# A two-layer hybrid backbone on one core: the mixed features are loaded into the slots of the split weights instead of the slots of the raw weights

## The chip, the core and the metric

The kernel runs on one core of one Trainium2 chip, as one program. The metric is the device time of one execution in microseconds (us), and the time of a kernel is the median over several executions. The engines of the core are called PE (matrix multiplication, with PEld for its weight loads), DVE (vector), ACT (scalar), POOL and SP. Each works through its own instructions strictly in the order in which the program holds them, and each instruction waits at the head of its engine for the semaphores that it needs. DMA transfers are issued by SP and ACT from that same order, so a transfer that has to wait holds up whatever stands behind it on that engine.

## The reference: what is computed

512 latent tokens and 256 context tokens of width 1024 go through two layers. Cut to what matters here:

```
for layer in range(DEPTH):                      # DEPTH = 2
    a   = modulate(rms_norm(h, norm1_g[layer]), shift1, scale1)
    p   = a @ w_in[layer]                       # one projection, columns shared out to three groups
    d   = diff_mixer(p ...)                     # differential attention, 256 columns
    q   = gqa_mixer(p ...)                      # grouped-query attention, 384 columns
    n   = gdn_mixer(p ...)                      # gated DeltaNet in both directions, 384 columns
    h   = h + gate1 * (concatenate([d, q, n]) @ w_out[layer])
    h   = h + gate2 * swiglu(modulate(rms_norm(h, norm2_g[layer]), shift2, scale2),
                             ffn_w_gu[layer], ffn_w_down[layer])
return rms_norm(h, final_norm_g)
```

In layer 0 the context tokens go through the same steps with their own modulation; in layer 1 they only serve as keys and values, so only the 512 latent tokens are mixed, projected and passed on. The change touches the step between the three mixers and `@ w_out`.

## The kernel before, in words

Activations lie transposed, as eight blocks of 128 features by tokens, numbered k = 0 to 7: k 0 and 1 come from the differential attention, k 2 to 4 from the grouped-query attention, k 5 to 7 from DeltaNet. Every large product is made in three passes over pairs of fp32r parts: a value is split into a high part (a copy, on ACT, L185) and a low part (value minus high part, on DVE, L161), and `mm3` (L194 on) multiplies hi by hi and hi by lo for every k and then lo by hi for every k (matmuls on L188; transposes are on L191).

**The mixers.** `mixers` runs a list of items in a fixed order for each layer, PLAN (L38): attention steps (`a`), DeltaNet inversions, scan steps and outputs (`p`, `s`, `o`), and near the end `x0`, which calls `mixed`. The order of the five attention pairs is HORD = (2, 0, 3, 1, 4), so k = 4 is finished last. `attn_post` (L1235) sends each finished pair to a DRAM buffer `mixd` (tile `OT`, issued by SP); `gdn_out` (L927) sends k 5 to 7 there (tile `z2`). The last pair, k 4, does not go through DRAM: it is transposed by PE into `otr` and split from there.

**The reload.** `mixed` (L958 to L970) loads the seven other blocks (`early_k`: k 0, 1, 2, 3, 5, 6, 7) from `mixd` into tiles `mx`, by SP (L152), and splits each into `mhi` and `mlo`. The split is made for each part of the tokens: in layer 0 the parts are 512 and 256 tokens, in layer 1 they are two of 256, so each `mx` has two copies on ACT and two subtractions on DVE.

**The region of the weights.** `mixed` also opens (L961, `open_a`, L1422) the region from which the out-projection takes its weights: slots of 128 by 1024 floats, 3 with the tag `raw`, 4 with `hi`, 4 with `lo`. A slot that is asked for again waits for the last reader of its old content. `wunit` (L212) takes one slot of each tag, loads 512 KB of weights into `raw` (by ACT's queue, L156), copies it to `whi` (ACT, L185) and subtracts to `wlo` (DVE, L161). In the kernel before, the seven `mx` tiles go round the three `raw` slots, so that the fourth `mx` waits for the first to be split, and the first weights `w_o` come after them in the same slots.

**The out-projection.** `outproj` makes eight column tiles `ops` for each part, each of 24 products (seven blocks of `mx` with three products each, then three for k 4), and adds each to the residual stream `h`, which has been in DRAM meanwhile and is loaded back by SP behind the `mx` loads. Two PSUM banks take turns, so a third tile waits until the first has been added to `h` on DVE. The norm, the gate and up products (`guc`, `gu`) and the down products (`dps`) follow.

The order on each engine is not that of the Python text: a scheduler goes over the whole program with its own estimates of time, and puts each engine's instructions in the order in which it finds them ready, with priorities for weights and for the mixers.

Of the kernel before, what the change touches and what calls it, by code (L numbers as in the profile page):

```python
# [10 lines left out]
F32 = mybir.dt.float32  # L11
# [83 lines left out]
class Net:  # L95
# [862 lines left out]
    def mixed(self, l, side, parts):  # L958

        self.G2.close()  # L960
        self.G.close()  # L961
        self.open_a(l + 1, side)
        tags = "ce" if l == DEPTH - 1 else "ac"
        self.mhi, self.mlo = ([self.ablock(n, *p[:2], t) for p, t in zip(parts, tags)] for n in ("mhi", "mlo"))
        t0 = min(p[0] for p in parts)
        for kt in self.early_k(l):
            x = self.W.slot("mx", F32, "raw")
            self.dma(x[:, t0:TOK], self.mixd[kt][:, t0:TOK])
            for a, n, _ in parts:
                self.split(self.at(self.mhi, kt, a, n), self.at(self.mlo, kt, a, n), x[:, a:a + n])  # L970
# [695 lines left out]
```

## Time and profile before

| | kernel before |
|---|---|
| time, median of 3 runs | 2184.11 us (2183.25 to 2184.77) |
| the profiled execution: its time | 2187.43 us |
| its span in the trace | 2185.6 us |
| busy: PE, PEld | 92%, 77% of the span |
| busy: DVE, ACT, POOL | 61%, 38%, 24% |
| mean granted clock of PE | 0.943 |

A page of the profile shows one execution. Times are in us from the start of the span; "x7" after an instruction means that seven like it stand in one row. In a list in order of time, the square brackets hold how long the engine stood idle before the row, and what released it; a duration is from start to end, and matmuls overlap, so a steady rate is read from the distance of the starts. The granted clock is given as a share of full speed: 1.00 is 2.4 GHz, 0.50 is 1.2 GHz, and a value between is a stretch with some of each.

### The profile page before, as it was taken

How to read it: one execution, taken by the hardware profiler on the slowest of the kernel's cores; microseconds unless marked ns; L12 is line 12 of the kernel's file. 1: busy time of each engine (PE TensorE's matmuls, PEld its weight loads, DVE VectorE, ACT ScalarE, POOL GpSimd, SP SyncE). 2: the span in 40 equal slices, each digit the busy share in tenths (PEclk: the TensorE clock that was granted, in tenths of full speed). 3: DMA queues.
4: the chain of work that ended last, by engine and by line, in shares of the span. 5: the costliest groups of instructions: out<-in, count | busy, mean ns of one | idle time of the engine just before them, and what ended most of it. 6: DMA issues, size and time to landing. Idle time of an engine off the chain costs nothing. (4 is left out here: it accounts for less than half of the span.)

```text
span 2185.6 us, 36979 instructions
## 1 busy us (share of the span) xinstructions
PE 2020.9 (92%) x14786; PEld 1672.6 (77%) x14786; DVE 1325.2 (61%) x2223; ACT 823.8 (38%) x1609; POOL 525.0 (24%) x768
## 2 busy tenths in 40 slices
PE   7999877998889999999999989977899799999998
PEld 3788766776668888888888888865676598888887
DVE  6755774575845747565757457687767664443444
ACT  5433315464744321212122344423475653222223
POOL 2403579331014100000000350367323030000002
PEclk9999987698999999999999989987798999999999
DMA  8354434221062324343424411444212242222321
GB/s 296 121 176 132 156 109 113 47 73 35 26 227 78 116 87 154 110 131 102 155 91 140 134 56 48 133 127 125 51 47 60 86 165 77 100 85 92 106 98 61
DMA packets 167596, 236.46 MB, mean 108 GB/s; under 512 B 75328, under 2 KB 109248, under 8 KB 167424
## 3 DMA queue, kind: packets, MB, share of 16 engines
q10 hardware_dynamic: 46160, 144.92, 20.2%
q1 hardware_dynamic: 121264, 89.18, 13.4%
q8 instruction: 116, 1.90, 0.3%
q14 instruction: 56, 0.46, 0.1%
HBM read 198.00 MB, written 36.04 MB: 107 GB/s over the span
## 5 line engine op out<-in xcount | busy, mean ns | idle before, releaser
L185 ACT ACTIVATE whi<-raw 128x1024 fp32r<-128x1024 f32 (+4 forms) x246 | 220.7, 912 | 499.6 <-PE dps L188 207.3
L161 DVE TENSOR_TENSOR wlo<-raw,whi 128x1024 fp32r<-128x1024 f32 (+4 forms) x236 | 250.1, 1074 | 222.1 <-ACT whi L185 221.3
L188 PE MATMUL gu<-ahi,wlo 128*128 128x512 f32 x672 | 264.0, 393 | 1.1 <-DVE wlo L161 1.1
L188 PE MATMUL gu<-ahi,whi 128*128 128x512 f32 x672 | 263.6, 392 | 0.0
L188 PE MATMUL dps<-acth,whi 128*128 128x512 f32 (+1 forms) x560 | 186.6, 348 | 0.4 <-DVE h L179 0.2
L188 PE MATMUL dps<-acth,wlo 128*128 128x512 f32 (+1 forms) x560 | 185.7, 346 | 0.0
L188 PE MATMUL gu<-alo,whi 128*128 128x512 f32 x672 | 168.9, 392 | 0.0
L179 DVE SCALAR_TENSOR_TENSOR junk<-adaw,cb 128x1024 bf16<-128x1024 f32 x112 | 136.8, 1222 | 37.6 <-DMA adaw<-ada_t 36.6
L188 PEld LDWEIGHTS gu<-ahi,wlo 128*128 128x128 f32 x672 | 126.5, 188 | 28.3 <-DVE wlo L161 1.5
L188 PE MATMUL tps<-whi,ahi 128*128 128x512 f32 (+4 forms) x368 | 137.9, 379 | 11.1 <-ACT dq L185 7.2
L188 PEld LDWEIGHTS gu<-alo,whi 128*128 128x128 f32 x672 | 126.3, 188 | 27.6
L179 DVE SCALAR_TENSOR_TENSOR h<-dps,md,h 128x512 f32<-128x512 f32 (+1 forms) x128 | 80.6, 633 | 109.6 <-PE dps L188 109.3
L188 PEld LDWEIGHTS gu<-ahi,whi 128*128 128x128 f32 x672 | 126.5, 188 | 26.7
L188 PE MATMUL tps<-wlo,ahi 128*128 128x512 f32 (+4 forms) x368 | 138.3, 376 | 2.6 <-DVE wlo L161 2.4
L161 POOL TENSOR_TENSOR md<-md,adab 128x2 f32<-128x2 f32 x56 | 32.0, 572 | 439.5 <-DVE junk L179 439.5
L188 PE MATMUL tps<-whi,alo 128*128 128x512 f32 (+4 forms) x368 | 137.3, 373 | 0.0
L1161 DVE TENSOR_REDUCE nm<-S 128x1 f32<-128x768 f32 (+1 forms) x140 | 117.0, 844 | 32.6 <-PE S L188 31.4
L182 ACT ACTIVATE P<-S,nm 128x768 f32<-128x768 f32 (+1 forms) x140 | 114.0, 815 | 51.7 <-DVE nm L1161 46.1
L161 POOL TENSOR_TENSOR sqc<-sqc 128x256 f32<-128x256 f32 x35 | 35.4, 1012 | 397.8 <-ACT sqc L182 397.4
L188 PE MATMUL dps<-actl,whi 128*128 128x512 f32 (+1 forms) x560 | 124.3, 346 | 0.0
L188 PEld LDWEIGHTS dps<-acth,whi 128*128 128x128 f32 x560 | 105.4, 188 | 15.6 <-DVE h L179 0.4
L188 PEld LDWEIGHTS dps<-acth,wlo 128*128 128x128 f32 x560 | 105.7, 189 | 14.3
(295 smaller groups left out, 4629.0 us busy)
## 6 DMA issues: line engine op xcount, KB each, us to landing
raw<-w_u ACTq DMA_DIRECT2D x88, 512.0 KB
adaw<-ada_t ACTq DMA_DIRECT2D x56, 512.0 KB
adaw<-ada_p ACTq DMA_DIRECT2D x24, 512.0 KB
raw<-w_o ACTq DMA_DIRECT2D x24, 512.0 KB
raw<-w_d ACTq DMA_DIRECT2D x44, 256.0 KB
raw<-w_d ACTq DMA_DIRECT2D x32, 320.0 KB
adaq<-ada_q SPq DMA_DIRECT2D x16, 512.0 KB
raw<-w_t ACTq DMA_DIRECT2D x16, 512.0 KB
```

The source lines that it names most:

```text
L161: (eng or self.v).tensor_tensor(out=out, in0=a, in1=b, op=op)
L179: self.v.scalar_tensor_tensor(out=out, in0=a, scalar=sc, in1=b, op0=op0, op1=op1, **k)
L182: self.s.activation(out=out, in_=in_, func=func, **k)
L185: self.s.activation(out=out, in_=in_, func=AF.Copy, **k)
L188: self.t.matmul(out, lhsT, rhs, start=start, stop=stop)
L1161: self.v.tensor_reduce(out=nm, in_=pin, axis=AX.XY if nk == 768 else AX.X, op=ALU.max, negate=True)
```

## The change

`mixed` asks for its seven slots by another tag: in turn `hi` and `lo`, where it asked for `raw`. So k 0, 2, 5 and 7 fill the four `hi` slots and k 1, 3 and 6 fill three of the four `lo` slots, and no `mx` waits for another. The three `raw` slots are empty, and the first three weight loads of the out-projection find them so. In exchange the first `whi` and `wlo` tiles come behind `mx` tiles: the second `whi` follows k 2 and the second `wlo` k 1, the third `whi` k 5, the third `wlo` k 3. The number of instructions is the same on every engine.

```
     def mixed(self, l, side, parts):
...
-        for kt in self.early_k(l):
-            x = self.W.slot("mx", F32, "raw")
+        for i, kt in enumerate(self.early_k(l)):
+            x = self.W.slot("mx", F32, ("hi", "lo")[i % 2])
             self.dma(x[:, t0:TOK], self.mixd[kt][:, t0:TOK])
             for a, n, _ in parts:
                 self.split(self.at(self.mhi, kt, a, n), self.at(self.mlo, kt, a, n), x[:, a:a + n])
```

Other slots move the scheduler's estimates, and with them the order on all engines: besides the places below, some 600 rows on PE and some 300 each on DVE and ACT stand elsewhere than before in layer 1, most of them in the DeltaNet and attention work between about 1490 and 1740 us of the trace; POOL's order is the same.

First the loads of layer 1 on SP, at the end of the mixers; rows with - stood there before, rows with + stand there now. In the names, `mx_17566` is k 0, `mx_17572` k 1, `mx_17578` k 2, `mx_17584` k 3, `mx_17590` k 5, `mx_17596` k 6, `mx_17602` k 7, and each `OT` is a finished attention pair on its way to DRAM (`mixd1`).

```order
 L152 DMA mx_17566<-mixd1_14856 128x512
+L152 DMA mx_17578<-mixd1_14856 128x512
+L152 DMA mx_17590<-mixd1_14856 128x512
+L152 DMA mx_17602<-mixd1_14856 128x512
 L152 DMA mixd1_14856<-OT_17052 128x512
 L152 DMA mixd1_14856<-OT_17518 128x512
 L152 DMA mx_17572<-mixd1_14856 128x512
-L152 DMA mx_17578<-mixd1_14856 128x512
 L152 DMA mx_17584<-mixd1_14856 128x512
-L152 DMA mx_17590<-mixd1_14856 128x512
 L152 DMA mx_17596<-mixd1_14856 128x512
-L152 DMA mx_17602<-mixd1_14856 128x512
```

The four blocks that go to the `hi` slots moved ahead of the two waits for attention pairs; k 1, 3 and 6 stay behind the second pair, which is k 1 itself.

The same moment of layer 1 on ACT, whose queue issues the weights. Before, the first weight load stood some sixty rows later; in the changed order it reads:

```order
L185 ACTIVATE PT_16863<-pt_16869 128x384
L156 DMA raw_17779<-w_o 128x1024
L156 DMA raw_17813<-w_o 128x1024
L156 DMA raw_17848<-w_o 128x1024
L185 ACTIVATE OTs_16889<-pv_16876 128x128
L185 ACTIVATE PT_16913<-pt_16914 128x384
L182 ACTIVATE P_16978,Z_16974<-S_16975,nm_16979 128x768
L182 ACTIVATE P_16985,Z_16974<-S_16982,nm_16986 128x768
L185 ACTIVATE mhi_17534<-mx_17566 128x256
```

And the end of the mixers on ACT, where the out-projection starts. Before:

```order
L185 ACTIVATE OTs_17724<-pv_17711 128x128
L185 ACTIVATE mhi_17540<-mx_17596 128x256
L185 ACTIVATE mhi_17548<-mx_17596 128x256
L156 DMA raw_17779<-w_o 128x1024
L185 ACTIVATE mhi_17541<-mx_17602 128x256
L185 ACTIVATE mhi_17549<-mx_17602 128x256
L185 ACTIVATE mhi_17538<-otr_17728 128x256
L156 DMA raw_17813<-w_o 128x1024
L156 DMA raw_17848<-w_o 128x1024
L185 ACTIVATE whi_17780<-raw_17779 128x1024
```

and in the changed kernel:

```order
L185 ACTIVATE PT_17698<-pt_17704 128x384
L185 ACTIVATE whi_17814<-raw_17813 128x1024
L185 ACTIVATE mhi_17547<-mx_17590 128x256
L185 ACTIVATE mhi_17540<-mx_17596 128x256
L185 ACTIVATE OTs_17724<-pv_17711 128x128
L185 ACTIVATE mhi_17548<-mx_17596 128x256
L185 ACTIVATE mhi_17541<-mx_17602 128x256
L185 ACTIVATE mhi_17549<-mx_17602 128x256
L156 DMA raw_17918<-w_o 128x1024
L185 ACTIVATE whi_17849<-raw_17848 128x1024
L185 ACTIVATE whi_17884<-raw_17883 128x1024
```

The first three weight loads are gone from here, the first `whi` was made in the middle of the attention, and the second `whi` stands among the last `mx` copies; the loads that stand here now are those of later tiles.

On PE in layer 0, at the same junction, `ops` is a column tile of the out-projection, `otr` the transposes of the last attention pair (k 4), `pv` the end of its attention. Before:

```order
L191 MATMUL otr_6845<-ident_92,O_6429 128x128 x4
L188 MATMUL pv_6836<-PT_6817,gV_3481 64x128
L191 MATMUL otr_6852<-ident_92,O_6429 128x128
L188 MATMUL pv_6836<-PT_6829,gV_3481 64x128
L188 MATMUL pv_6836<-PT_6817,gV_3481 64x128
L188 MATMUL pv_6836<-PT_6829,gV_3481 64x128
L188 MATMUL ops_6920<-mhi_6639,whi_6915 128x512
L191 MATMUL pv_6836<-ident_92,OTs_6841 128x128
L188 MATMUL ops_6920<-mhi_6639,wlo_6916 128x512
```

and in the changed kernel, at the end of the tile's 14 products with `mhi`:

```order
L188 MATMUL ops_6920<-mhi_6646,whi_6915 128x512
L188 MATMUL ops_6920<-mhi_6646,wlo_6916 128x512
L191 MATMUL otr_6845<-ident_92,O_6429 128x128 x4
L191 MATMUL otr_6852<-ident_92,O_6429 128x128
L191 MATMUL pv_6836<-ident_92,OTs_6841 128x128
L188 MATMUL ops_6920<-mlo_6655,whi_6915 128x512
```

In layer 0 the fourteen products moved ahead of the last pair's transposes; before, five of the six `otr` transposes came ahead of the tile and the last one behind its fifth `mlo` product. In layer 1 PE now runs two column tiles without k 4 and makes the k 4 products of both behind them, where each tile had its own at its end.

## Rows read from the trace of the kernel before

**Rows 1.** Chain that ended last, layer 1: start, us, what.

```profile
1730.81 2.00 DMA mixd<-OT
1732.82 2.61 DMA mx<-mixd
...
1740.80 6.90 DMA raw<-w_o
...
1748.81 1.24 DVE wlo L161
...
1750.09 29.73 PE ops L188 x228
...
1825.85 44.62 PE gu L188 x192
```

**Rows 2.** PE in order of time, start of the out-projection of layer 1.

```profile
1740.86 0.33 PE L191 MATMUL otr<-ident,O 128*128 128x128 f32 x1 [0.38 <-DVE O L161]
1748.83 0.58 PE L188 MATMUL ops<-mhi,whi 128*128 128x256 f32 x1 [7.65 <-ACT whi L185]
1750.09 0.58 PE L188 MATMUL ops<-mhi,wlo 128*128 128x256 f32 x1 [0.68 <-DVE wlo L161]
...
1755.06 0.28 PE L188 MATMUL ops<-mhi,whi 128*128 128x256 f32 x1
...
1757.94 0.28 PE L188 MATMUL ops<-mhi,whi 128*128 128x256 f32 x1
```

**Rows 3.** ACT in order of time, same place (ACTq: DMA issues of its queue).

```profile
1735.46 0.72 ACT L185 ACTIVATE mhi<-mx 128x256 fp32r<-128x256 f32 x2 [3.25 <-DMA mx<-mixd]
...
1736.61 1.33 ACT L185 ACTIVATE mhi<-mx 128x256 fp32r<-128x256 f32 x4
1738.00 0.49 ACT L185 ACTIVATE PT<-pt 128x384 f32<-128x384 f32 x1
...
1739.83 0.26 ACT L185 ACTIVATE OTs<-pv 128x128 f32<-128x128 f32 x1
...
1742.00 1.02 ACTq L156 DMA_DIRECT2D raw<-w_o  x2
1747.72 1.06 ACT L185 ACTIVATE whi<-raw 128x1024 fp32r<-128x1024 f32 x1 [5.38 <-DMA raw<-w_o]
```

**Rows 4.** Stretches: length, busy by engine, granted PE clock, DMA share, GB/s.

```profile
1490.00:1540.00 50.00, 34.47 (x532) 26.93 (x533) 35.99 (x74) 22.84 (x53) 30.39 (x48) 0.76 0.53 137
1540.00:1600.00 60.00, 51.81 (x816) 38.12 (x816) 40.87 (x82) 28.96 (x68) 20.79 (x25) 0.77 0.19 39
...
1688.00:1700.00 12.00, 9.90 (x72) 6.54 (x72) 10.42 (x19) 9.23 (x22) 0.00 (x0) 1.00 0.08 23
...
1736.00:1741.00 5.00, 3.03 (x25) 1.87 (x21) 3.44 (x10) 3.60 (x12) 0.00 (x0) 1.00 0.59 190
1741.00:1749.00 8.00, 0.35 (x2) 0.17 (x1) 1.96 (x6) 2.62 (x7) 0.00 (x0) 0.52 0.93 338
1749.00:1755.00 6.00, 5.32 (x24) 5.03 (x25) 3.73 (x4) 2.06 (x3) 0.00 (x0) 0.51 0.88 290
```

**Rows 5.** ACT in order of time, the same junction of layer 0.

```profile
611.32 0.94 ACT L185 ACTIVATE mhi<-mx 128x512 fp32r<-128x512 f32 x2 [2.25 <-DMA mx<-mixd]
...
627.75 0.38 ACT L185 ACTIVATE mhi<-otr 128x256 fp32r<-128x256 f32 x1 [1.85 <-PE otr L191]
```

**Rows 6.** PE in order of time, the out-projection of layer 0.

```profile
621.95 0.50 PE L188 MATMUL ops<-mhi,whi 128*128 128x512 f32 x1 [0.69 <-ACT whi L185]
...
623.21 0.50 PE L188 MATMUL ops<-mhi,wlo 128*128 128x512 f32 x1 [0.65 <-DVE wlo L161]
...
627.44 0.27 PE L191 MATMUL otr<-ident,O 128*128 128x128 f32 x1
...
635.66 0.47 PE L188 MATMUL ops<-mhi,whi 128*128 128x512 f32 x1 [1.28 <-DVE h L179]
```

**Rows 7.** DVE in order of time, layer 0: the residual sums.

```profile
634.76 1.41 DVE L179 SCALAR_TENSOR_TENSOR h<-ops,md,h 128x512 f32<-128x512 f32 x2 [3.53 <-DMA h<-h]
```

**Rows 8.** SP's DMA issues in order of time, layer 0.

```profile
627.74 4.95 SPq L152 DMA_DIRECT2D h<-h  x8
```

More of the change, by code (lines that the diff above doesn't have):

```diff
@@ L965, in mixed @@
         t0 = min(p[0] for p in parts)
-        for kt in self.early_k(l):
-            x = self.W.slot("mx", F32, "raw")
+        for i, kt in enumerate(self.early_k(l)):
+            x = self.W.slot("mx", F32, ("hi", "lo")[i % 2])
             self.dma(x[:, t0:TOK], self.mixd[kt][:, t0:TOK])
```

## The prediction

> **What bounds the kernel now.** I read the chain of waits first, for the work that sets the end. In layer 1 it leaves the engines at the end of the mixers: from the write of the last attention pair through DRAM, over the `mx` loads, to the load of the first out-projection weights, which takes 6.90 us, then the low part of those weights, and only then PE [rows 1]. From there PE carries the chain on, and at 1825.85 it is still PE, in the gate and up products [rows 1]. So what is saved ahead of 1750.09 should reach the end. Next, PE in order of time: it finishes the last transpose at 1740.86 + 0.33 = 1741.19 and stands idle for 7.65 us, released by `whi`, and 0.68 more for `wlo` [rows 2]. Then ACT, which would make `whi`: it waits 5.38 us for the weights [rows 3]. Nothing else is due there. The weights are late only because their slot was an `mx` tile's until just before. Last, the stretches: in the idle one the DMA share is 0.93 at 338 GB/s, and the granted clock, 1.00 in the five us before it, is 0.52; it is still 0.51 in the six us behind it, with PE busy for 5.32 of them [rows 4]. So the first tile's 24 products, from 1748.83 to 1755.06, ran at the lower level (1.2 GHz), and the second tile took 1757.94 - 1755.06 = 2.88 us, 0.12 a product, at the upper one (2.4 GHz) [rows 2]. At half speed 0.12 becomes 0.24; the first group shows about (1755.06 - 1750.09) / 23 = 0.22 each.
>
> **Layer 1, what is removed.** Before, two column tiles are through at 1757.94 [rows 2]. After, the three weight loads are issued in the stretch 1688 to 1700, where the DMA share is 0.08 [rows 4], some 40 us before they are needed, so they are there. The next limit is the chain that the change leaves alone: pair k 1 must come back through DRAM, so ACT's first copy of it still starts at 1735.46 [rows 1, 3]. From there ACT has to make 12 copies for six blocks, by 1.33 / 4 = 0.33 each 4.0 us, and in the same order one `PT` of 0.49, two `OTs` of 0.26 and one `whi` of 1.06 [rows 3]: 6.1 us in all, so the copies are made by about 1741.5. That k 2 and k 5 are now loaded earlier gives nothing, since ACT's order puts them behind k 1. PE has no more wait on weights and can run the tiles from about 1741.5, a moment after its own last transpose. It has 42 products for two tiles without k 4, and six for k 4: 48. At 0.12 that is 5.8 us, ending at 1747.3; at 0.22 it is 10.5 us, ending at 1752.0. Against 1757.94 that saves between 6.0 and 10.7 us. Which of the two is a matter of the clock: it falls in the stretch in which PE works for 0.35 of 8.00 us [rows 4], and this stretch disappears, but the five us before have PE busy for only 3.03 and still show 1.00 [rows 4]. That is nearer to full speed, so I take 9.3 of the 6.0 to 10.7. Later tiles need a weight load each in 2.88 us at full clock; 512 KB at 338 GB/s [rows 4] is 1.55 us, so they keep pace, with the fourth tile's load now issued before the mixers are over.
>
> **Layer 1, what is added.** In the attention before it, ACT issues three transfers, by 1.02 / 2 = 0.51 each 1.5 us, and makes one `whi` of 1.06 us [rows 3], 2.6 us in all. ACT is busy for 9.23 of 12.00 us there, DVE for 10.42 and PE for 9.90 [rows 4], so none of them alone is full; part of ACT's extra work falls in its gaps. The bounds are 0 and 2.6; I take 1.3. The `wlo` of 1.24 us [rows 1] stands on DVE just ahead of the k 1 subtractions, while DVE waits for the copies from `mx`; nothing. Layer 1 then gives 9.3 - 1.3 = 8 us, between 6.0 - 2.6 = 3.4 and 10.7.
>
> **Layer 0.** The same junction costs less, since the weights come almost in time: PE waits 0.69 us for `whi` and 0.65 for `wlo` [rows 6]. But ACT had stood still for 2.25 us for an `mx` that waited for a `raw` slot [rows 5], and this goes. PE was free for the tile at 621.95 - 0.69 = 621.26; without the two causes it starts there or up to 2.25 earlier, at 619.0 to 621.3. Now the order matters: the 14 products with `mhi` run ahead of the last pair's transposes. With twice the columns of layer 1 a product is 0.24 us by 0.12, so they end at 622.4 to 624.7; five transposes and one of `pv` at about 0.2 (from 0.33 and 0.27 with overlap [rows 2, 6]) add 1.2, seven `mlo` products 1.7. The last transpose then comes at 625.3 to 627.6 against 627.44 [rows 6]. It releases the loads of `h`: SP issued all eight at 627.74, in the same moment as ACT's copy from it at 627.75 [rows 5, 8]. DVE waits for `h` until 634.76, PE's third tile for DVE until 635.66 [rows 6, 7]. So what PE gains in the first two tiles is lost again unless `h` comes earlier, and the gain is that of the transpose, -0.2 to 2.1 us, plus what `h` wins if fewer weights are in flight with it; as the upper end I let it win another 2.25. In the attention ahead of it the 1.5 us of issues and 1.06 of `whi` stand against the 2.25 us of ACT's wait that is gone, about even. The bounds are -0.2 and 4.4; I take 2.
>
> **The moved order.** The other rows that change places in layer 1 are the same work in another order. PE is busy for 34.47 + 51.81 = 86.3 us of the 110 from 1490 to 1600 [rows 4], so 23.7 us of idle time is the most that a better order could give back; a worse one could add as much. With nothing in the rows to lean on either way I take 0, and 4 us either way for the range.
>
> **Sum.** 8 + 2 = 10 us. The profiled execution, at 2187.4 us, would become 2177.4; it stood 3.3 us above the median of the runs shown, 2184.1, of which 2174.1 is left. I say 2174. A difference below 0.2%, 4.4 us, can't be told from none here: the bounds of the three signs are 2179.7 and 2188.5.
>
> **Rivals.** *The lower clock stays.* If the first tiles of layer 1 still run at 1.2 GHz, 6.0 us is left there, less 1.3 of extra work, and layer 0 may give 1: 5.7 us in all, 2178.4. For it speaks that the clock was still 0.51 with PE busy for 5.32 of 6.00 us [rows 4]; against it, that the cause of the fall, the long wait, is gone.
>
> *The waits only move.* The weight loads stand on ACT ahead of the first `mx` copy and the first `whi` stands between two probabilities, while SP now issues four `mx` loads at once beside them. If the three loads of 512 KB are served ahead of the `mx`, ACT stands behind them for up to 1.57 MB / 338 GB/s [rows 4] = 4.65 us a layer, 9.3 us in both, in attention where PE, DVE and ACT wait for each other; 10 less 9.3 leaves 0.7, 2183.4. Against it speaks the DMA share of 0.08 in that stretch [rows 4], which leaves the loads alone there. The Trainium skill, "DMA: Bandwidth & Descriptors", section "Issuing engines are not separate DMA queues", says that transfers issued by different engines go over the same hardware DMA engines, so that issuing from ACT doesn't get the weights past SP's loads. The trace agrees, since the weights took 6.90 us where the eight `h` loads were in flight [rows 1].
>
> *Slower.* The moved order costs PE its clock in the DeltaNet stretch. From 1490 to 1600 the mean granted clock is 0.766, weighted by busy time [rows 4]. If it came down to 0.65, the same 86.3 us would be 86.3 x 0.766 / 0.65 = 101.7, 15.4 more, and 10 saved leaves 5.4 lost: 2189.5. It takes over from a clock of about 0.69, where the 10 us are used up. For it speaks that PE's clock is split between its levels just there; against it, that the same products in the same stage leave PE as much work as before.
>
> **How the numbers follow.** The forecast has 0.53, its own range being about 2168 to 2179.5; the lower clock 0.24, the moved waits 0.13, slower 0.10. Faster by over 0.2%: nearly all of the forecast and some nine tenths of the lower clock, 0.74. Slower: 0.09 of the last. The rest, 0.17, is within 0.2%. At its lower end the range takes 10.7 in layer 1 and most of 4.4 in layer 0 with a good part of the 4 us of the order, 2166; at its upper end it goes almost to the moved waits, 2183. Two in ten are left to both sides together.
>
> **What would show it.** In the trace after, PE should start the out-projection of layer 1 within a us or two of its last transpose, with no wait on `whi`, and two tiles should be through 6 to 11 us after it, with the granted clock telling which. ACT's wait for `mx` in layer 0 should be gone, and `h` there should be issued 0 to 2 us sooner. From 1490 to 1676 the start of each stage should lie within 4 us of before. The prediction is wrong if ACT's first copy of k 1 in layer 1 no longer starts about 1735, if `whi` in the attention waits for its load, or if PE's busy time in the DeltaNet stretch grows.

## The result, and the profile after

The changed kernel takes 2171.23 us in the median of five runs (2165.54 to 2174.47), the kernel before 2184.77 beside it (2183.25 to 2187.01): a ratio of 0.9932, 95% interval 0.9919 to 0.9946, or 13.5 us. Forecast were 2174 and 10 us. The profiled execution took 2171.23 us, its span is 2169.4.

The loads of weights are out of the way. This is PE in order of time at the start of the out-projection of layer 1 in the changed kernel; it answers to [rows 2].

```profile
1733.78 0.38 PE L188 MATMUL ops<-mhi,whi 128*128 128x256 f32 x1
1734.55 0.33 PE L191 MATMUL pv<-ident,OTs 128*128 128x128 f32 x1 [0.39 <-ACT OTs L185]
1735.04 0.39 PE L188 MATMUL ops<-mhi,wlo 128*128 128x256 f32 x1 [0.16 <-DVE wlo L161]
...
1741.49 0.39 PE L188 MATMUL ops<-mhi,whi 128*128 128x256 f32 x1 [0.46 <-DVE h L179]
```

The wait of 7.65 us for `whi` is gone; the longest one left in the row is 0.46. The third column tile starts at 1741.49; ACT, in order of time, had begun with k 1 at 1729.61 (answering to [rows 3]):

```profile
1729.61 0.42 ACT L185 ACTIVATE mhi<-mx 128x256 fp32r<-128x256 f32 x1 [3.24 <-DMA mx<-mixd]
...
1732.66 1.06 ACT L185 ACTIVATE whi<-raw 128x1024 fp32r<-128x1024 f32 x1
```

So from the first copy of k 1 to the third tile it takes 11.9 us, where it took 1757.94 - 1735.46 = 22.5 [rows 2, 3]: 10.6 us saved. And the clock stays up; the columns are length, busy time by engine, granted clock of PE, DMA share and GB/s, as in [rows 4]:

```profile
1725.00:1735.00 10.00, 8.04 (x73) 5.58 (x72) 6.98 (x15) 6.38 (x20) 0.00 (x0) 1.00 0.74 247
1735.00:1741.00 6.00, 5.96 (x48) 5.79 (x48) 5.02 (x11) 3.34 (x7) 0.00 (x0) 1.00 0.77 245
1741.00:1749.00 8.00, 7.54 (x63) 7.51 (x63) 5.29 (x7) 4.45 (x7) 2.15 (x2) 1.00 0.70 243
```

The two traces are 2185.6 - 2169.4 = 16.2 us apart, more than the medians. To see where, one needs marks that sit alike in every kernel. POOL's order is the same in all of them but d3, so its rows serve. These are the five of the changed kernel, in order of time: the second of the two `drs` of layer 0's attention (A), the first `md` behind layer 0's out-projection (B), the first of the two `drs` of layer 1 (C), the last `ors` of the DeltaNet outputs (D), and the last `drs` (E), which belongs to k 1 and stands just ahead of the junction.

```profile
586.62 2.27 POOL L161 TENSOR_TENSOR drs<-rsqd,mhalf 128x12 f32<-128x12 f32 x1 [76.29 <-DVE rsqd L176]
...
733.77 0.19 POOL L161 TENSOR_TENSOR md<-md,adab 128x2 f32<-128x2 f32 x1 [17.11 <-DVE junk L179]
...
1643.11 1.65 POOL L161 TENSOR_TENSOR drs<-rsqd,mhalf 128x8 f32<-128x8 f32 x1 [5.22 <-DVE rsqd L176]
...
1671.08 2.72 POOL L161 TENSOR_TENSOR ors<-rsqo,mhalf 128x6 f32<-128x6 f32 x2 [0.93 <-DVE rsqo L176]
1720.59 1.64 POOL L161 TENSOR_TENSOR drs<-rsqd,mhalf 128x8 f32<-128x8 f32 x1 [46.79 <-DVE rsqd L176]
```

In the kernel before the same rows start at 591.27, 738.83, 1645.20, 1677.49 and 1726.43. The lengths of the six stages, for these two and for the profiles of all experiments below, in us:

| kernel | start to A | A to B: junction of layer 0 | B to C | C to D: end of DeltaNet | D to E: last attention | E to end: junction of layer 1 |
|---|---|---|---|---|---|---|
| before | 591.3 | 147.6 | 906.4 | 32.3 | 48.9 | 459.2 |
| changed | 586.6 | 147.2 | 909.3 | 28.0 | 49.5 | 448.8 |
| c1, changed again | 588.5 | 146.2 | 908.9 | 28.0 | 48.9 | 449.1 |
| e2, changed, third | 591.4 | 147.0 | 909.1 | 28.0 | 51.6 | 448.8 |
| c2, layer 0 only | 588.7 | 147.2 | 906.7 | 28.0 | 47.2 | 459.2 |
| c3, layer 1 only | 588.7 | 147.7 | 909.8 | 31.3 | 47.8 | 448.2 |
| c4, layer 1, weights late | 584.4 | 148.2 | 906.1 | 32.3 | 47.7 | 454.4 |
| d1, before, wait filled | 592.0 | 147.0 | 909.8 | 31.6 | 48.1 | 456.8 |
| d2, loads behind k 0 | 594.3 | 145.8 | 908.2 | 28.0 | 50.3 | 450.1 |
| d3, transposes first | 588.2 | 145.3 | 915.5 (C moved) | 24.5 (C moved) | 59.0 | 448.6 |
| d4, k 1 without DRAM | 594.0 | 146.0 | 907.5 | 28.0 | 54.0 | 447.9 |
| e1, both layers' moves | 588.4 | 151.3 | 909.9 | 28.0 | 47.1 | 448.9 |
| f1, layer 1's moves | 591.2 | 145.8 | 905.0 | 28.0 | 48.1 | 448.7 |

In d3 the row C stands four rows later in POOL's order than in the others, so that only the sum of its two stages from B to D, 939.9, can be set beside theirs: 937.3 in the changed kernel.

Three readings. The first stage holds no moved instruction, and still spreads from 584 to 594: 4.7 of the 16.2 us between the two profiles lie there and are not the change's. The last stage has two values, 459.2 with the old slots in layer 1 and 448.2 to 449.1 with the new ones, apart from c4, d1, d2 and d4, whose edits reach into it; and it doesn't care for layer 0: some 10.3 us. And a third term stands in C to D, where no slot is touched: 31.3 to 32.3 with the old slots in layer 0, 28.0 with the new ones. B to C, 905.0 to 909.9 without d3, has a mean of 908 with either.

### The profile page after: what moved, and what is told of

It reads as the page before. It is cut to its first block, busy times and chain, and to the rows that moved or that the text cites. A ratio compares the mean times of both kernels' runs of the same rounds, so it can differ in the third digit from the quotient of the medians.

```text
span 2169.4 us, 36961 instructions
## 1 busy us (share of the span) xinstructions
PE 2009.9 (93%) x14786; PEld 1663.1 (77%) x14786; DVE 1324.6 (61%) x2223; ACT 822.3 (38%) x1609; POOL 527.6 (24%) x768
## 3 DMA queue, kind: packets, MB, share of 16 engines
q1 hardware_dynamic: 121264, 89.18, 13.5%
```

## The experiments

**c1, e2: the changed kernel again.** No edit; on two chips, each beside runs of the kernel before.

> The changed kernel once more, beside the three parts of it. Theory 1 (the saved time lies at the two junctions): 10 to 13.5 us below the kernel before, and in its trace the gain is at the start of the out-projection of layer 1, 10 us, and next to none in layer 0. Theory 2 (part of the measured 13.5 us is the granted clock of earlier stretches, in which no instruction has moved): up to 585 us of the trace the two kernels have the same order, so the place where the traces part by 4.7 us ahead of that moves from one execution to the next, by 0 to 5 us either way.

> The changed kernel a third time, on the same chip as the run before it. By the parts seen so far: 10.5 us at the junction of layer 1, 0.4 to 1.4 at that of layer 0, 4.9 between 1660 and 1680 us from the moved order, less 1.3 to 1.9 in the attention behind it: 13 to 16 below the kernel before, of which the clock of stretches with the same order moves 3 us either way.

Measured: 0.9939 (0.9923 to 0.9955) and 0.9935 (0.9920 to 0.9950). The ratio holds on both. The first stage was 588.5 and 591.4 us against 586.6 in the first profile of the same program, so theory 2 holds for the profiles: a difference of 5 us between two single traces can lie where nothing moved. Of theory 1 the junction of layer 1 holds, 10.2 us in c1; that the junctions are all of the gain does not, as c2 shows.

**c2: layer 0 only.**

```
-            x = self.W.slot("mx", F32, ("hi", "lo")[i % 2])
+            x = self.W.slot("mx", F32, ("hi", "lo")[i % 2] if l == 0 else "raw")
```

> The new slots in layer 0 alone; layer 1 keeps the raw slots. It also carries most of the moved order in layer 1's DeltaNet work, since that comes from the earlier end of layer 0 in the scheduler's estimates. By the forecast's term: 2 us faster. By the trace of the changed kernel: 0.3 us faster, PE starting the out-projection about 1 us earlier but at the lower clock. If the moved order is worth something, it shows here as a shift between 1490 and 1676 us, within 4 us either way.

Measured: 0.9962 (0.9948 to 0.9976), 8.3 us, far above the 2 us forecast for layer 0 and above the 0.3 of the trace. The table shows why. The junction of layer 0 gives 0.4 us here; C to D gives 4.3. This is the moved order. Kernel before, four stretches around the end of the DeltaNet work of layer 1, with the columns of [rows 4]; the forecast did not look there:

```profile
1655.00:1660.00 5.00, 4.99 (x96) 4.03 (x92) 3.11 (x7) 3.47 (x9) 2.33 (x4) 1.00 0.35 88
1660.00:1665.00 5.00, 3.29 (x35) 2.43 (x36) 4.21 (x11) 1.09 (x3) 3.57 (x4) 0.78 0.31 74
1665.00:1670.00 5.00, 5.00 (x42) 3.45 (x44) 2.64 (x6) 1.08 (x2) 0.00 (x0) 0.50 0.00 0
1670.00:1675.00 5.00, 5.00 (x44) 3.68 (x43) 3.05 (x6) 0.60 (x1) 0.00 (x0) 0.50 0.01 3
```

The changed kernel in the same place:

```profile
1660.00:1665.00 5.00, 5.00 (x44) 3.02 (x43) 4.47 (x11) 2.02 (x4) 2.61 (x2) 1.00 0.00 1
1665.00:1670.00 5.00, 4.70 (x48) 3.52 (x47) 4.81 (x10) 3.01 (x7) 1.82 (x2) 1.00 0.01 3
```

Before, PE waits 1.35 us for a `kT` from DVE and 0.34 for POOL, and then works without a gap at 0.50 of its clock, the lower level (1.2 GHz), for ten us. PE in order of time, kernel before:

```profile
1661.70 0.73 PE L188 MATMUL stk<-kT,pick 32*128 32x512 f32 x2 [1.35 <-DVE kT L161]
```

With the new order it waits 0.23 and 0.34 us for other tiles there, and the clock stays at 1.00. PE in the changed kernel:

```profile
1657.82 0.33 PE L915 MATMUL ops<-X,qK 128*64 128x64 f32 x2 [0.23 <-DVE X L161]
1658.49 0.92 PE L901 MATMUL scan<-X,kdec 128*64 128x64 f32 x24 [0.34 <-DVE X L161]
```

It is no single execution's luck: all four traces with the old order have the wait of 1.35 us, the lower clock behind it, and 31.3 to 32.3 us in this stage; all eight with the new slots in layer 0 that keep the changed kernel's DeltaNet order have neither, and 28.0. That the wait brings the clock down isn't shown by that: in the same four traces PE waits 1.32 us for another tile 13 us ahead, and the clock stays at 1.00 behind it, in the kernel before from 1648 to 1660.

```profile
1648.55 0.55 PE L191 MATMUL pt<-ident,P 128*128 128x128 f32 x3 [1.32 <-DVE PT L1196]
```

**c3: layer 1 only.**

```
+            x = self.W.slot("mx", F32, ("hi", "lo")[i % 2] if l == 1 else "raw")
```

> The new slots in layer 1 alone; all that stands ahead of the last attention of layer 1 keeps the order of the kernel before. By the forecast's term: 8 us faster, all of it between the end of the attention and the third column tile. By the trace of the changed kernel: 10 to 10.6. If the clock of the moved DeltaNet order made the gain, only 3 to 5 us.

Measured: 0.9941 (0.9924 to 0.9958), 12.9 us with 3.7 either way. The last stage is 11.0 us shorter, D to E 1.1, C to D 1.0, so by the trace the junction gives what the changed kernel showed, and the order of the DeltaNet work, which is that of the kernel before here, gives next to nothing.

The two halves don't add up: 8.3 and 12.9 us are 21, where the whole change gives 13.5, and the three intervals of 3 to 4 us each hardly cover that. Some 4 us of the difference stand in D to E, where c2 saves 1.8 and c3 1.1 us while the changed kernel loses 1.1 in the mean of its three traces. Where the rest lies isn't shown.

**c4: layer 1 only, the weights late.** The wait is taken apart: `mx` loads free of each other, the first three weight loads behind the copies of k 6 by an edge in ACT's order.

```
+            if kt == 6:
+                self.mark = self.lastcp.ins
...
+            with (self.tc.issue_after(mark.ins) if mark is not None else ExitStack()):
                 self.wdma(raw[:, :n] if c == 1 else ...
```

> As the run with the new slots in layer 1 alone, but the first three weight loads of the out-projection are issued on ACT only behind the copies of k 6, where the kernel before had its first one: the mx loads are free of each other, the weights come late. If the late weights were the whole loss: within 2 us of the kernel before, with PE idle for 6 to 8 us ahead of the first column tile at the same place and a clock near 0.5 there. If the mx loads that waited for each other were part of it: 3 us or more faster than before.

Measured: 0.9975 (0.9964 to 0.9986), 5.5 us; the last stage is 454.4, 4.8 below the kernel before and 6.2 above c3. The first expectation fails and the second holds: the `mx` loads that no longer wait for each other are worth nearly half of it. PE in c4, in order of time:

```profile
1733.44 0.33 PE L191 MATMUL otr<-ident,O 128*128 128x128 f32 x1 [0.38 <-DVE O L161]
1737.07 0.58 PE L188 MATMUL ops<-mhi,whi 128*128 128x256 f32 x1 [3.30 <-ACT whi L185]
1738.33 0.58 PE L188 MATMUL ops<-mhi,wlo 128*128 128x256 f32 x1 [0.68 <-DVE wlo L161]
```

The wait for `whi` is 3.30 us where it was 7.65. The copies of k 6 come earlier, since its load no longer waits for another block's slot, and so the weight loads start earlier, 1730.44 - 1718.75 = 11.7 us behind mark E where it was 1740.80 - 1726.43 = 14.4. But a wait of 3.30 us costs the clock as one of 7.65 does: it is 0.50 behind it.

```profile
1735.00:1741.00 6.00, 3.25 (x13) 2.96 (x14) 3.63 (x4) 3.60 (x5) 0.00 (x0) 0.50 0.78 259
```

**d1: the kernel before, its wait filled.** This measures the clock by itself: 56 products ahead of the first column tile, whose sum is overwritten.

```
             ps = self.mm_bank("ops")
+            if l == 1 and not kept0 and ct == 0:
+                for j in range(56):
+                    self.mm(ps[:, :n], self.at(self.mhi, 7, t0, 128), self.at(self.mhi, 7, t0, n))
```

> The kernel before with 56 products more, whose result is overwritten: they stand on PE behind the last transpose of layer 1 and ahead of the first product of the out-projection, 56 x 0.12 = 6.7 us in the 7.65 us in which PE waited for the weights. Nothing waits for them. If the fall of the clock in that wait is part of what the wait cost: the first column tile runs at the upper level, 0.12 a product in place of 0.22, and the kernel gains 2.2 to 2.5 us without any change of the loads. If the clock does not depend on it: no gain, or a loss of up to 1 us.

Measured: 0.9989 (0.9971 to 1.0007), 2.4 us, which the interval doesn't part from none. The trace does: the last stage is 456.8, 2.4 us shorter, and PE runs the first column tile at full rate.

```profile
1743.92 6.98 PE L188 MATMUL ops<-mhi 128*128 128x256 f32 x56 [0.56 <-ACT mhi L185]
...
1751.75 0.39 PE L188 MATMUL ops<-mhi,wlo 128*128 128x256 f32 x1 [0.73 <-DVE wlo L161]
1751.97 0.28 PE L188 MATMUL ops<-mhi,whi 128*128 128x256 f32 x1
```

So of the 10.3 us at the junction 2.4 are the clock that the wait took down, and some 8 the wait itself. By the trace the first expectation holds.

**d2: the weight loads of layer 1 behind the first `mx`.** The same edge as in c4, on the changed kernel, with the mark at k 0. It asks what the early loads cost.

> The changed kernel, with the first three weight loads of layer 1 put behind the copies of k 0 on ACT instead of ahead of them; the rest of the order is nearly the same. In the changed kernel the mx of k 0 took 6.1 us to land and ACT stood 2.40 us for it. If the three weight loads cause that: the landing comes down to about 2.6 us, ACT waits under 0.7 us, and the kernel is 1.3 to 2 us below the changed one. If it is only the four mx loads at once: no change.

Measured: 0.9937 (0.9921 to 0.9952), which is the changed kernel's time. In the changed kernel the chain of waits holds the landing of k 0:

```profile
1679.76 6.10 DMA mx<-mixd
```

with the three weight loads, issued on ACT at 1678.03 and 1678.40, in flight beside it; ACT stands for it:

```profile
1678.03 0.33 ACTq L156 DMA_DIRECT2D raw<-w_o  x1
...
1678.40 0.93 ACTq L156 DMA_DIRECT2D raw<-w_o  x2
...
1685.88 0.72 ACT L185 ACTIVATE mhi<-mx 128x256 fp32r<-128x256 f32 x2 [2.40 <-DMA mx<-mixd]
```

That wait is 1.09 and 3.35 us in the other two traces of the same kernel. In d2 the same four `mx` loads are issued at once, but the weights only when k 0 is there. The chain of waits holds its landing again:

```profile
1684.88 2.63 DMA mx<-mixd
```

ACT doesn't wait for the `mx`, but now the first `whi` is at the head of its queue before its weights have come, between two probabilities:

```profile
1687.54 0.34 ACTq L156 DMA_DIRECT2D raw<-w_o  x1
...
1687.91 0.93 ACTq L156 DMA_DIRECT2D raw<-w_o  x2
...
1693.70 1.06 ACT L185 ACTIVATE whi<-raw 128x1024 fp32r<-128x1024 f32 x1 [2.17 <-DMA raw<-w_o]
```

The loads were the cause of the late landing, as the first theory had it; but its gain of 1.3 to 2 us didn't come, since the wait only moved. The Trainium skill, "DMA: Bandwidth & Descriptors", section "Issuing engines are not separate DMA queues", says that loads issued from two engines share the hardware DMA engines. These traces agree, with 6.10 us beside 2.63.

**d3: the last transposes first, in layer 0.** The products of the column tiles get an edge behind the last transpose of the last pair.

```
+            with (self.tc.issue_after(self.lasttr.ins) if l == 0 else ExitStack()):
                 self.mm3(ps[:, :n], ... early_k(l)], stop=False)
```

> The changed kernel, with the transposes of the last attention pair ahead of the first column tile in layer 0, as in the kernel before, so that h is loaded about 5 us sooner. If the late load of h is what takes the gain of layer 0 away: 1 to 2 us below the changed kernel. If PE itself is the bound there, at its lower clock: within 1 us, or up to 1.5 us above it, since PE idles until the last pair is ready.

Measured: 1.0000 (0.9989 to 1.0012): all 13 us are lost again, which neither theory had. The junction of layer 0 is not to blame; it is the shortest of all, 145.3. `h` is issued at 620.09 there, 5 us ahead of c1's 625.13, and only 0.9 us less is needed than in c1. The loss stands in layer 1, where the edit has no line: B to E takes 999.0 us, against 986.8 in the changed kernel. The edit changes the scheduler's estimates, and with them the order of the DeltaNet and attention work, on POOL too. Of the 12.2 us 2.6 lie from B to D. d3, two stretches of that:

```profile
1580.00:1600.00 20.00, 17.64 (x270) 13.61 (x268) 12.17 (x21) 12.56 (x31) 2.29 (x3) 0.83 0.07 12
1600.00:1620.00 20.00, 17.91 (x337) 14.82 (x335) 9.04 (x16) 13.05 (x30) 1.61 (x2) 0.83 0.19 55
```

The changed kernel shows a clock of 1.00 in both. The other 9.5 us lie in D to E, the last attention, where ACT in d3 stands for PE and then for the first `mx`:

```profile
1687.66 0.28 ACT L185 ACTIVATE OTs<-pv 128x128 f32<-128x128 f32 x1 [4.18 <-PE pv L188]
...
1691.47 0.72 ACT L185 ACTIVATE mhi<-mx 128x256 fp32r<-128x256 f32 x2 [2.65 <-DMA mx<-mixd]
```

In the changed kernel the same two waits are 1.22 and 2.40 us. The clock of the stage is 0.88 against 0.93; what makes up the rest of the 9.5 isn't shown. So a moved order alone is worth 12 us the wrong way here and 3.9 us the right way in the changed kernel.

**d4: k 1 of layer 1 without DRAM.** `x0` stands ahead of `a9` in PLAN, and `attn_post` splits the finished pair into `mhi` and `mlo`.

```
-        "... w0 o2 a8 a9 x0 a10"
+        "... w0 o2 a8 x0 a9 a10"
...
-                    self.attn_post(l, *prev)
+                    self.attn_post(l, *prev, split=parts if l == 1 and prev[0] == 1 else None)
```

> The changed kernel, with k 1 of layer 1 split straight from its finished pair, like k 4, instead of through DRAM and back; the other six blocks are loaded as before. If the way of k 1 through DRAM is the next limit: ACT's wait of 3.24 us for its mx is gone, the first column tile starts 2.5 to 3.2 us sooner, and the kernel is that much below the changed one. If ACT's copies are the limit: under 1 us. The moved order may add 2 us either way.

Measured: 0.9942 (0.9925 to 0.9958), no better than the changed kernel. The wait of 3.24 us is gone and the last stage is 0.9 us shorter, the second theory's figure. D to E is 54.0 us against 48.9 to 51.6: the copies that filled idle time at the end now stand in the attention, and there DVE is full and the clock down.

```profile
1710.00:1720.00 10.00, 7.63 (x37) 5.73 (x37) 10.00 (x20) 9.46 (x22) 0.00 (x0) 0.67 0.46 160
```

**e1, f1: the first copy of weights later.** e1 takes d2's edge in both layers, puts layer 1's first `whi` behind a later query tile of the attention (an edge behind the thirteenth `OTs` copy of that layer), and in layer 0 the first four `otr` transposes of the last pair ahead of the tiles. f1 takes only the two moves of layer 1.

```
+            with (self.tc.issue_after(wm) if wm is not None else ExitStack()):
                 self.cp(hi[:, :n], raw[:, :n])
```

> The changed kernel with three moves that leave the DeltaNet order of layer 1 as the changed kernel has it: the first three weight loads of both layers behind the copies of k 0; in layer 1 the first copy of weights two query tiles later, when its load has landed; in layer 0 five of the six transposes of the last pair ahead of the first column tile. If the waits of ACT for mx (2.40 us) and for the first weights (2.17 us in the run with the loads alone moved) are what the attention of layer 1 lost: 1.5 to 2.5 us less between 1680 and 1725 us, and about 1 us less at the junction of layer 0, so 2.5 to 3.5 us below the changed kernel. If DVE and PE bound the attention anyway: under 1 us.

> The changed kernel with the two moves of layer 1 alone: the first three weight loads behind the copies of k 0, the first copy of weights two query tiles later; layer 0 is as the changed kernel has it. In the run that also moved layer 0, the attention of layer 1 lost nothing (-0.6 us from 1680 to 1725, against +1.9, +1.3 and +4.0 in three traces of the changed kernel), and layer 0 lost 3.8 by its own moves. If both hold: ACT waits for neither, that stretch loses under 0.5 us, layer 0 gives its 0.4 to 1.4 us, and the kernel is 2 to 4 us below the changed one, 15 to 18 below the kernel before.

Measured: e1 0.9943 (0.9927 to 0.9959), f1 0.9904 (0.9889 to 0.9919). In e1 D to E is 47.1, 1.8 to 4.5 us below the changed kernel's three traces, as expected; but its moves in layer 0 cost 4 to 5 us (A to B 151.3), and of the 2.5 to 3.5 us that were to come nothing is left. f1 keeps the good half: 48.1 and 145.8. ACT waits for neither load in it:

```profile
1681.55 0.82 ACTq L156 DMA_DIRECT2D raw<-w_o  x2
1682.41 0.45 ACTq L156 DMA_DIRECT2D raw<-w_o  x1
1682.48 0.73 ACT L185 ACTIVATE mhi<-mx 128x256 fp32r<-128x256 f32 x2
...
1688.09 1.06 ACT L185 ACTIVATE whi<-raw 128x1024 fp32r<-128x1024 f32 x1
```

With a median of 2168.4 us against 2188.6 for the kernel before beside it, f1 is ahead of both kernels; the three ratios of the changed kernel are 0.9932 to 0.9939. Its B to C, 905.0, is the shortest of all, and no edit is there, so of its 20 us some 3 are not the edit's. In D to E, where the edit stands, it is 1.9 us below the changed kernel's mean of 50.0.

## Why the prediction was right, step by step

**The bound.** Right. The chain into the out-projection of layer 1 was the weights' load, behind a slot that an `mx` held, and what was saved there reached the end: 10.3 us by the mean of the changed kernel's three last stages, 448.9, against 459.2. What the prediction didn't take apart c4 does: 4.8 us come with the `mx` loads alone, before any weight is loaded earlier than the copies of k 6 allow.

**Layer 1, removed.** Taken were 9.3 us of 6.0 to 10.7. Measured: 10.6 in the first profile, the upper end. The next limit was named rightly, ACT's copies from the start of k 1: twelve of them, two `OTs`, a `PT` and a `whi` were to take 6.1 us; with a second `PT` they take 5.8. The open point was the clock, and it stayed at 1.00. d1 gives the part of it: 2.4 us, which the wait had cost beside its length.

**Layer 1, added.** Taken were 1.3 of 0 to 2.6 us, as ACT's work. D to E went from 48.5 (mean of before and d1) to 50.0 in the mean of the three traces, 1.5 us, but for another reason: not the issues and the copy, which f1 has too and pays nothing for, but ACT's wait for the `mx` behind the weight loads, 1.09 to 3.35 us. The stage grows with this wait: 47.8 us at 0.66 (c3), then 48.9 at 1.09, 49.5 at 2.40 and 51.6 at 3.35. Set beside c2, which has the changed kernel's DeltaNet order without the early loads, 47.2, the cost is 2.8. The second rival, the waits that only move, was right in its mechanism in layer 1, and at 4.65 us it was priced too high.

**Layer 0.** Taken were 2 us of -0.2 to 4.4. Measured: 1.1, from 147.6 (mean of the four traces with the old slots there) to 146.4 (mean of the seven with the changed kernel's layer 0). The step that failed is the rate of the products. They were costed at 0.24 us each; in the first profile ten of the first fourteen start 0.4 to 0.6 us apart.

```profile
616.30 0.80 PE L188 MATMUL ops<-mhi,whi 128*128 128x512 f32 x1
616.89 0.63 PE L188 MATMUL ops<-mhi,wlo 128*128 128x512 f32 x1
...
620.71 0.40 PE L188 MATMUL ops<-mhi,whi 128*128 128x512 f32 x1
```

The first rival, the lower clock, was said of layer 1; it came true here instead. The changed kernel:

```profile
605.00:610.00 5.00, 2.85 (x31) 2.04 (x32) 5.00 (x13) 5.00 (x12) 0.00 (x0) 1.00 0.00 1
610.00:615.00 5.00, 2.79 (x17) 1.49 (x14) 4.50 (x9) 1.91 (x4) 0.00 (x0) 0.54 0.61 210
615.00:620.00 5.00, 5.00 (x17) 3.86 (x18) 0.40 (x2) 0.28 (x1) 0.00 (x0) 0.50 0.31 105
```

ACT and DVE are busy for 5.00 of 5.00 us in the first row, mostly with the copies and low parts of the landed blocks and of the weights: the `mx` wait of 2.25 us did go, and the engine that had waited became the bound. PE is idle for almost half of the ten us, and the clock falls. But it falls at this junction in the kernel before too, where PE waited 2.05 us:

```profile
612.76 1.33 PE L191 MATMUL pt<-ident,P 128*128 128x128 f32 x5 [2.05 <-ACT P L182]
...
610.00:615.00 5.00, 2.31 (x18) 1.50 (x14) 2.65 (x8) 2.20 (x6) 0.00 (x0) 0.65 0.55 161
615.00:620.00 5.00, 4.29 (x27) 2.59 (x25) 3.28 (x9) 2.91 (x7) 0.00 (x0) 0.67 0.58 190
```

There it was back at 1.00 when the tile began; the changed kernel begins its tile 1.0 us sooner, counted from mark A, and inside the low stretch. How much of the tile falls into it differs between executions of the same instructions: ten slow products in the first profile, nine in e2, four in c1. Where none to three are slow (d4, d2, f1), A to B is 145.8 to 146.0, near the 2 us taken. With the old slots c3 has ten slow products and d1 eight, the kernel before and c4 none. So the low clock isn't the new slots' doing alone, and what ends it sooner or later isn't shown.

`h` was to be issued 0 to 2 us sooner. Counted from mark A it is issued 37.6 us behind it in the first profile, against 36.5: 1.1 later. What came sooner is its landing. DVE's first sum with it stands 628.21 - 624.22 = 4.0 us behind the issue, against 634.76 - 627.74 = 7.0, which is the term that the prediction let in only for its upper end. With the old slots c3 has 4.8 there, so the slots alone don't make it.

```profile
628.21 0.75 DVE L179 SCALAR_TENSOR_TENSOR h<-ops,md,h 128x512 f32<-128x512 f32 x1 [0.97 <-DMA h<-h]
```

**The moved order.** Taken was 0, with 4 us either way, since no row spoke for a side. It gave 3.9 us, from 31.9 in C to D to 28.0. This is the term that most of the 3.5 us between forecast and result come from: 10.3 + 1.1 + 3.9 - 1.5 = 13.8 from the stages, and 13.5 measured. The bound of 4 us was too narrow as a rule; in d3 a moved order cost 12 us, most of it in the last attention. The third rival, slower by the clock of the DeltaNet stretch, had the mechanism, and the sign fell the other way for this kernel. It also looked at the wrong stretch: from 1490 to 1600 the clock is 0.77 before and 0.78 after, and what changed lies from 1660 on.

**The signs.** One sign of being wrong came true: ACT's first copy of k 1 starts at 1729.61 and not about 1735. It was set in the time of the trace, which had moved; behind mark E the copy starts 1729.61 - 1720.59 = 9.0 us, and before 1735.46 - 1726.43 = 9.0, so the chain that it was to guard stayed as it was. Another held only in part: the stages from 1490 to 1676 were to start within 4 us of before, and C is 2.1 us earlier, but D, at the end of them, 6.4. One reading was wrong: beside the load of 6.90 us the prediction has eight `h` loads in flight, which [rows 1] don't show. SP issued the last three of the eight only when that load had landed, at 1740.80 + 6.90 = 1747.70:

```profile
1747.71 1.41 SPq L152 DMA_DIRECT2D h<-hd  x3
```

**The sum.** So the time was within the range for a part of the wrong reasons: layer 1 as reckoned, layer 0 at half its term, and nearly a third of the gain from an order that the change moved by accident.

What stays open: why just these rows of DeltaNet changed places isn't shown, only what it did; why the two layers apart give more than together; and the change's slots were tried only as they are, not with all `mx` tiles in `hi`.

## What to carry to other kernels

A buffer that two stages share sets when the second stage's loads may start; read for each slot who held it last, and move the short-lived tiles to slots that are asked for late. Loads that come free earlier also go into someone else's queue: put their issue behind the transfer that is needed first, and the first instruction that reads them behind the moment at which they land. And where a scheduler orders the whole program, compare stages by marks whose order doesn't move, since a change may win or lose more in a stage that it never touches than where it was made.

## What was not expected of the hardware

The clock of PE fell behind a wait of 3.30 us (c4) as far as behind one of 7.65, and in the DeltaNet work, in all four traces with the old order, after waits of 1.35 and 0.2 to 0.3 us within a busy stretch, to 0.50 for over ten us while PE was busy throughout; with waits of 0.23 and 0.34 it stayed at 1.00 in all eight traces with the new one, and also behind the wait of 1.32 us that stands 13 us ahead in the old one. And single executions differ by up to 10 us in the first 590 us, where the thirteen traces lie between 584.4 and 594.3 with no instruction moved. The clock goes with it: over the first 584 us it is 0.92 in the shortest (c4) and 0.89 in the longest (d2).
